# The output projection's products in another order, row sums in small pieces, most output blocks finished on VectorE

## The chip, the core and the metric

The kernel runs on one core of a Trainium2 chip. The core has five engines with a queue of instructions each: TensorE (PE in the profile; its weight loads are PEld), VectorE (DVE), ScalarE (ACT), GpSimd (POOL) and SyncE (SP). DMA transfers are issued from these queues. The metric is the device time of one execution in microseconds; the time before is the median of three runs.

## The reference, cut to what matters

One encoder layer over 1024 new frames of one stream (the prompt tokens) and 16 next frames of 8 running streams (the sample), in float32, model width 2048, eight stick-breaking heads and eight retention heads of 128.

```python
h = rms_norm(x, norm_pre)
q_sb, k_sb, v_sb, gate_sb, q_r, k_r, v_r, gate_r = project(h, w_in, pos)   # 2048 x 8192; rotary on q_r, k_r
o_sb = stick_breaking(q_sb, k_sb, v_sb)            # causal, prompt in blocks of 128, sample over a cache of 1024
o_r, state = retention(q_r, k_r, v_r, state)       # chunks of 64, per-head decay
y = concat(head_rms_norm(o_sb) * g_sb * silu(gate_sb), head_rms_norm(o_r) * g_r * silu(gate_r))
out = einsum('bte,ed->btd', y, w_out)              # 2048 x 2048, the output projection
x = x + rms_norm(out, norm_post)
return x, new keys and values, new states          # for prompt and sample
```

## The kernel before, in words

**Precision.** TensorE multiplies in a reduced float32. Every operand is therefore split: ACT copies it to the reduced type (`hi`, for weights `wh`, L139), DVE subtracts that from the original (`lo`, `wl`, L140), and a product is three matmuls, hi by wh, hi by wl and lo by wh.

**Stages.** The prompt has eight tiles of 128 tokens. Tiles 0–3 and the sample's tile form group 0, tiles 4–7 group 1. For each group the input projections run head by head (L314, L373, L401), in a written order of steps such as ("rk", 6), the retention keys of head 6. Attention and retention of a head are jobs: generators that are advanced by `tick`, one tick for each few matmuls, so that their instructions are mixed into the stream of projections. The number that a job yields is the count of ticks to its next piece. A job `column_sums` prepares sums of output weights in DRAM (`s_t`), a job `row_sums` sums of token operands. `place` keeps an instruction behind the product last issued, in the order that the scheduler then writes; an instruction without it stands where the scheduler puts it. Weights come on SP's queue into four buffers (`wr`), four splits ahead of use at most. Row sums, operand loads, input rows and accumulating outputs go on POOL's queue.

**Output projection.** It is done with seven products in place of eight for a 2 x 2 arrangement of blocks (tokens 0–3 and 4–7 by two columns blocks of 512), with sums of weights and of tokens. A unit is one such arrangement: `half` says which four heads of both branches are summed over, `u` which two column blocks; there are four units. Their seven products are named by digits: "1" uses operand a11 (tokens 0–3, stick-breaking heads), "2" a12 (tokens 0–3, retention heads), "4" a22 (tokens 4–7, retention heads), and "6", "5", "7" and "3" use sums S2, S1, s3 and s4 of such operands. One product is a step: 4 weight blocks by 4 token tiles by 3 matmuls, 48 matmuls of 128 x 512, in four PSUM banks. In all 28 steps (L1285), of which steps 0 and 1 follow the last input projections directly.

Between steps `fill` loads the next operand into a free slot by a 1 MB transfer, and two steps or more later, by the table `due`, `cut` splits it (L1261 on ACT, L1262 on DVE). When a tile of a step is complete, `give` adds its bank to the output blocks (`outs[t][c]`, tile t, column c, 128 x 512): copies on ACT, additions on DVE (L1384, and L1382 where the sign is turned). After its last product, a block is squared on ACT and multiplied by the gain on DVE (L1388). When the sum of squares of a tile is known, `scale` finishes the block: either on DVE (L1398), which multiplies by the scale and adds the input rows `xr` and sends the block by SP, or, where `added` says so, on ACT, with a transfer that adds onto rows which `give_x` has copied to the output before. `finish_first` does this for tokens 0–3; for tokens 4–7 it is done tile by tile as `mixed_last` interleaves the last unit's "7" and "4". `finish_sample` does the sample's rows (L1454): it loads a raw row block `rawc`, waits for its next turn and finishes it. The names `mh`, `ml`, `s3h`, `a22l` and so on in the trace are the hi and lo of operand slots.

The functions that the change touches, and what calls them:

## Time and profile before

| | |
|---|---|
| Time, median of 3 runs | 2340.72 us (2336.19 to 2345.64) |
| Profiled execution, its own time | 2345.99 us |
| Span of its trace | 2344.3 us |
| TensorE busy | 2276.5 us, 97% |
| DVE, ACT, POOL busy | 1410.7, 918.9 and 561.8 us |
| Transfers | 477.25 MB, mean 204 GB/s |

The span runs from the first to the last instruction of the profiled execution. A line such as `PE a L1285 <- DVE wl L140: 6.4, 4, 4.4` says that matmuls of line 1285 into `a` waited 6.4 us in all, 4 times, at most 4.4 us, for line 140 on DVE. In a timeline, each row has its start, its duration, engine, line and operation, output and inputs, and in brackets how long the engine had stood before and what released it. For DMA the last number is the microseconds from issue to landing.

### The profile page before, as it was taken

What the parts mean: (1) busy time and instruction counts of PE and PEld (TensorE: products, weight loads), DVE (VectorE), ACT (ScalarE), POOL (GpSimd) and SP (SyncE); (2) the same over time, 40 slices, a digit from 0 to 9 for tenths busy, and PEclk for the clock granted to TensorE, in tenths of its full rate; (3) what the DMA queues carried; (4) which work ended last, traced back from release to release, by engine and by line L of the source; (5) the groups of instructions that cost most, each with busy time, mean ns of one, the idle gap of its engine ahead of it and who ended that gap; (6) DMA issues with size and microseconds to landing.
All of it is one profiled execution on the core that took longest, in us unless ns stands there. A gap on an engine that the chain in (4) does not pass through costs nothing.

```text
span 2344.3 us, 38591 instructions
## 1 busy us (share of the span) xinstructions
PE 2276.5 (97%) x13920; PEld 2016.2 (86%) x13920; DVE 1410.7 (60%) x2763; ACT 918.9 (39%) x1899; POOL 561.8 (24%) x819
## 2 busy tenths in 40 slices
PE   7999999999999999999999999999998999999994
PEld 7999999999999999998888888888887787888873
DVE  8246564556555563556667766676665556745666
ACT  6323332333333242334443444444443443544333
POOL 2123241414223241313221321122022212100011
PEclk9999999999999999999999999999999999999997
DMA  7659786877869787798968888787769757685576
GB/s 250 158 142 229 167 184 170 189 194 175 203 149 203 173 190 183 175 222 222 219 190 230 243 238 252 232 255 225 230 190 255 195 146 206 237 242 200 170 234 178
DMA packets 702000, 477.25 MB, mean 204 GB/s; under 512 B 234960, under 2 KB 633552, under 8 KB 697200
## 3 DMA queue, kind: packets, MB, share of 16 engines
q1 hardware_dynamic: 623776, 317.32, 52.0%
q0 software_dynamic: 41968, 133.87, 21.7%
q10 hardware_dynamic: 36064, 23.60, 3.4%
q8 instruction: 109, 1.79, 0.3%
q14 instruction: 83, 0.68, 0.1%
HBM read 372.94 MB, written 117.44 MB: 209 GB/s over the span
## 4 chain that ended last, share of the span: by engine, by line
PE 82%; DMA 6%; issue 5%; DVE 4%; ACT 1%; POOL 1%; SPq 0%; DVEq 0%; POOLq 0%; ACTq 0%
PE acc L314 48%; PE accn L373 11%; PE a L1285 7%; PE accx L401 4%; PE pa L711 2%; PE z L678 2%; PE sao L1209 1%; PE pd L847 1%; PE zc L782 1%; DMA ml<-s_y 1%; DMA s_s<-s_S 1%; PE rs L869 1%; DMA be<-s_bd 1%; DMA s_S<-s_S 1%; PE pS L902 1%
## 5 line engine op out<-in xcount | busy, mean ns | idle before, releaser
L314 PE MATMUL acc<-mh,wh 128*128 128x256 f32 (+2 forms) x2304 | 662.1, 340 | 2.8 <-DVE rv L1162 1.8
L314 PE MATMUL acc<-ml,wh 128*128 128x256 f32 (+2 forms) x2304 | 662.8, 340 | 0.8 <-DVE p0u L152 0.8
L314 PE MATMUL acc<-mh,wl 128*128 128x256 f32 (+2 forms) x2304 | 663.5, 340 | 0.0
L140 DVE TENSOR_TENSOR wl<-wr,wh 128x512 fp32r<-128x512 f32 x432 | 296.3, 689 | 427.7 <-ACT wh L139 419.8
L139 ACT ACTIVATE wh<-wr 128x512 fp32r<-128x512 f32 x432 | 272.2, 632 | 588.1 <-PE acc L314 342.9
L314 PEld LDWEIGHTS acc<-mh,wh 128*128 128x128 f32 x2304 | 422.5, 188 | 39.5 <-issue 6.6
L314 PEld LDWEIGHTS acc<-mh,wl 128*128 128x128 f32 x2304 | 422.2, 189 | 36.7 <-issue 8.2
L314 PEld LDWEIGHTS acc<-ml,wh 128*128 128x128 f32 x2304 | 422.2, 188 | 35.9 <-issue 6.6
L763 POOL DMA_DIRECT2D kc<-cache_sb_k x256 | 167.1, 658 | 282.8 <-DVE kcT L794 130.2
L373 PE MATMUL accn<-whn,mh 128*128 128x256 f32 x768 | 223.9, 292 | 0.0
L373 PE MATMUL accn<-wln,mh 128*128 128x256 f32 x768 | 217.1, 283 | 0.0
L373 PE MATMUL accn<-whn,ml 128*128 128x256 f32 x768 | 217.0, 283 | 0.0
L373 PEld LDWEIGHTS accn<-whn,mh 128*128 128x128 f32 x768 | 146.7, 191 | 9.8 <-issue 7.9
L373 PEld LDWEIGHTS accn<-wln,mh 128*128 128x128 f32 x768 | 146.7, 191 | 0.3
L373 PEld LDWEIGHTS accn<-whn,ml 128*128 128x128 f32 x768 | 146.5, 191 | 0.0
L615 DVE TENSOR_TENSOR_SCAN kp<-kp 128x640 f32<-128x640 f32 (+6 forms) x72 | 108.4, 1505 | 37.0 <-POOL kp L604 34.4
L1285 PE MATMUL a<-wh,mh 128*128 128x512 f32 x320 | 124.7, 390 | 2.4 <-DVE o L1384 2.4
L1285 PE MATMUL a<-wl,mh 128*128 128x512 f32 x320 | 125.1, 391 | 1.7 <-DVE wl L140 1.7
L1285 PE MATMUL a<-wh,ml 128*128 128x512 f32 x320 | 125.1, 391 | 0.0
L587 DVE STREAM_TRANSPOSE kp<-be 128x640 f32<-128x640 f32 (+6 forms) x72 | 95.4, 1325 | 8.0 <-DMA be<-s_bd 6.0
L140 DVE TENSOR_TENSOR wln<-wrn,whn 128x512 fp32r<-128x512 f32 x80 | 54.9, 689 | 68.1 <-ACT whn L139 65.2
L139 ACT ACTIVATE whn<-wrn 128x512 fp32r<-128x512 f32 x80 | 50.6, 632 | 115.3 <-PE acc L314 59.2
(268 smaller groups left out, 3588.5 us busy)
## 6 DMA issues: line engine op xcount, KB each, us to landing
wr<-w_in SPq DMA_DIRECT2D x384, 256.0 KB, 4.6
vc<-cache_sb_v SPq DMA_DIRECT2D x64, 512.0 KB, 7.3
wr<-w_out SPq DMA_DIRECT2D x112, 256.0 KB, 4.0
wrn<-w_in SPq DMA_DIRECT2D x80, 256.0 KB, 3.8
kc<-cache_sb_k SPq DMA_DIRECT2D x256, 64.0 KB, 4.3
kc<-cache_sb_k POOLq DMA_DIRECT2D x256, 64.0 KB, 4.6
tr<-w_out SPq DMA_DIRECT2D x32, 512.0 KB, 6.5
s_t<-ts POOLq DMA_DIRECT2D x16, 1024.0 KB, 6.4
```

The lines of the kernel that those rows point to most:

```text
L139: nc.scalar.activation(hi, src, AF.Copy)
L140: nc.vector.tensor_tensor(lo, src, hi.bitcast(F32), ALU.subtract)
L314: last = nc.tensor.matmul(a[:, :m], lhs[:, j, :], rhs[w][:, j, o : o + m], start=(w == 0 and j == 0 and n == 0), stop=(w == KT // WQ - 1 a ...
L373: product[0] = nc.tensor.matmul(a, lhs[q][:, jj, ts], rhs[:, j, :], start=(w == 0 and j == 0 and n == 0 and t % 2 == 0), stop=(w == KT // ...
L401: product[0] = nc.tensor.matmul(banks[t], lhs[q][:, j, ts], rhs, start=(k == 0 and n == 0), stop=(k == KT - 1 and n == 2))
L587: place(nc.vector.transpose(dst.rearrange("p (k b j) -> p k j b", j=4, b=32), raw))
L615: nc.vector.tensor_tensor_scan(rev, rev, rev, 1.0, ALU.mult, ALU.bypass)
L678: mm = nc.tensor.matmul(z[:, :c], q2[a][:, i * P : (i + 1) * P], k2[b][:, :c], start=(m == 0), stop=(m == 2))
L711: nc.tensor.matmul(po[:, :P], at[:, j, :], rest["vn"][:, j, :], start=(j == 0), stop=(j == t))
L763: (nc.gpsimd if i < 2 else nc.sync).dma_start(kc[32 * i : 32 * i + 32, :].rearrange("p (k d) -> p k d", d=32), cache_k[0, 2 * c + j, s * 5 ...
L782: mm = nc.tensor.matmul(z[r, :], qp[:, j, r], ready[2 * j + c // 2][:, c % 2, :], start=(j == 0), stop=(j == 1),)
L1285: product[0] = nc.tensor.matmul(bank, a[:, k, ts], b, start=(name in "125" and k == 0 and n == 0), stop=(k == H // 2 - 1 and n == 2), skip ...
```

## The change

The order of the 28 steps is one list now. The units' products were "1625734", "1265734", "1265734", "1265374", unit after unit. Now the third unit stops after "12653", the fourth does "16532", and then come the third's "7" and "4" and the fourth's "7" and "4", so that the last four steps concern tokens 4–7 alone. The third unit's "7" and "4" start in a bank of their own, for which its "6" is given to three output blocks.

`s_t` is laid out so that one weight block is contiguous (rows of 2 KB one behind the other). `row_sums` goes head by head in pieces of 256 KB, waits for each head to be ended, and starts at head 4's keys in place of head 6's retention keys, 36 ticks between pieces, and for heads 4–7 12 ticks. `cut` is placed. Operand cuts come three steps after the fill. The sample's rows are finished during the second and third units, one turn longer after their load. `added` holds for the first column of tokens 0–3 only (4 blocks, 12 before), the other 28 blocks are finished on DVE; those of tokens 0–3 leave by POOL's queue, those of tokens 4–7 by SP's. The input rows for them come in pieces of 256 KB, five ticks apart.

```diff
 D_CS = 14
+D_RS = (36, 12)
...
-    s_t = [scr.tile([P, H, 4, 512], F32, name=f"s_t{u}") for u in range(2)]
+    s_t = [scr.tile([H, 4, P, 512], F32, name=f"s_t{u}") for u in range(2)]
...
-    UNITS = tuple(zip((0, 0, 1, 1), (0, 1, 0, 1), ("1625734", "1265734", "1265734", "1265374")))
+    STEPS = [(0, s) for s in "1625734"] + [(1, s) for s in "1265734"] + [(2, s) for s in "12653"]
+    STEPS += [(3, s) for s in "16532"] + [(2, s) for s in "74"] + [(3, s) for s in "74"]
...
-            last_load[0] = nc.sync.dma_start(wr, s_t[u][:, k, "5674".index(name), :])
+            last_load[0] = nc.sync.dma_start(wr, s_t[u][k, "5674".index(name)])
...
+            def ended(self):
+                return all("end" in x and x["end"].done for x in (self.rest, self.ret))
...
-                    place(nc.gpsimd.dma_start(s_t[u][:, k], t))
+                    place(nc.gpsimd.dma_start(s_t[u][k].rearrange("f p e -> p f e"), t))
...
-        def row_sums(q):
-            hs, hr = (slice(d * H + q * H // 2, d * H + (q + 1) * H // 2) for d in range(2))
+        def row_sums(q, wait):
+            heads = range(q * H // 2, (q + 1) * H // 2)
             for name, first, more in (
-                ("S2", s_sum["S1"][:, hs, :], s_y[0][:, hs, :NB_TOK]),
-                ("s3", s_y[0][:, hs, :NB_TOK], s_y[1][:, hs, :]),
-                ("s4", s_sum["S2"][:, hs, :], s_y[0][:, hr, :NB_TOK]),
+                ("S2", lambda h: s_sum["S1"][:, h, :], lambda h: s_y[0][:, h, :NB_TOK]),
+                ("s3", lambda h: s_y[0][:, h, :NB_TOK], lambda h: s_y[1][:, h, :]),
+                ("s4", lambda h: s_sum["S2"][:, h, :], lambda h: s_y[0][:, H + h, :NB_TOK]),
             ):
-                place(nc.gpsimd.dma_start(s_sum[name][:, hs, :], first))
-                yield D_TI[1]
-                place(nc.gpsimd.dma_start(s_sum[name][:, hs, :], more, accum_op=ALU.add))
-                yield D_TI[1]
+                for act, src in ((nc.gpsimd.dma_start, first), (add_rows, more)):
+                    for h in heads:
+                        while not ready[h]():
+                            yield 3
+                        place(act(s_sum[name][:, h, :], src(h)))
+                        yield wait
+                made.add((name, q))
+
+        made = set()
+        ready = {}
+
+        def add_rows(dst, src):
+            return nc.gpsimd.dma_start(dst, src, accum_op=ALU.add)
...
                 hi, lo = (x[:, j : j + 2, :NB_TOK] for x in mix[name])
-                nc.scalar.activation(hi, lo.bitcast(F32), AF.Copy)
-                nc.vector.tensor_tensor(lo, lo.bitcast(F32), hi.bitcast(F32), ALU.subtract)
+                place(nc.scalar.activation(hi, lo.bitcast(F32), AF.Copy))
+                place(nc.vector.tensor_tensor(lo, lo.bitcast(F32), hi.bitcast(F32), ALU.subtract))
...
-                if (gi, step, h) == (1, "rk", 6):
-                    run["rows"] = Job(row_sums(0), 2)
+                if (gi, step, h) == (1, "k", 4):
+                    run["rows"] = Job(row_sums(0, D_RS[0]), 2)
...
-            end = n == (2 if t >= 4 and c % 2 == 0 else 4)
+            end = n == (4 if t < 4 else {0: 3, 1: 5, 2: 2, 3: 4}[c])
...
-                nc.vector.scalar_tensor_tensor(o, o, rs, xrs[t, c // 2][:, c % 2 * 512 : (c % 2 + 1) * 512], ALU.mult, ALU.add)
-                nc.sync.dma_start(y_rows(t)[:, cs], o)
+                nc.vector.scalar_tensor_tensor(o, o, rs, xrs[t, c], ALU.mult, ALU.add)
+                (nc.gpsimd if t < 4 else nc.sync).dma_start(y_rows(t)[:, cs], o)
...
-            return c < 2 and t < 6
+            return t < 4 and c == 0
+
+        wanted = [(t, c) for t in range(PT) for c in range(4) if not added(t, c)]
+
+        def load_x(q):
+            for x in "hl":
+                xr = mp.tile([P, 5, 512], F32, name="xr", tag=f"m{x}{q}")
+                for j in range(5):
+                    if wanted:
+                        t, c = wanted.pop(0)
+                        place(nc.gpsimd.dma_start(xr[:, j], x_rows(t)[:, c * 512 : (c + 1) * 512]))
+                        xrs[t, c] = xr[:, j]
+                        yield 5
...
-            for t in range(6):
-                xs_given[t] = nc.scalar.dma_start(y_rows(t)[:, :1024], x_rows(t)[:, :1024])
+            for t in range(4):
+                xs_given[t] = nc.scalar.dma_start(y_rows(t)[:, :512], x_rows(t)[:, :512])
...
                 place(nc.gpsimd.dma_start(xr, xs_flat[:, cs]))
                 yield
+                yield
                 nc.vector.tensor_tensor(raw, raw, gpost[:, cs], ALU.mult)
...
+        banks = {(0, "1"): chain}
+        for step, (n, name) in enumerate(STEPS):
+            half, u = divmod(n, 2)
+            x1, x2 = 2 * u, 2 * u + 1
+            if (n, name) == (0, "2"):
+                job = Job(row_sums(1, D_RS[1]), 96)
+            if (n, name) == (2, "1"):
                 drain(job)
-            if n == 2:
                 given_x = Job(give_x(), 2)
-            pools = (accp, accq) if n % 2 == 0 else (accq, accp)
-            banks = {}
-            for name in names:
-                if step > 1:
-                    banks[name] = (
-                        four(pools[name in "25"]) if name in "125" else banks["1" if name in "674" else "5"]
-                    )
+            if n in (1, 2) and step < 20:
+                next(sample, None)
+            for combo in due.pop(step, ()):
+                cut(combo)
+            if step < 2:
+                continue
+            apart = n == 2 and name in "74"
+            if name in "125" or (apart and name == "7"):
+                pool = accq if name in "257" or n == 1 and name == "1" else accp
+                if n == 1 and name in "25":
+                    pool = accp
+                banks[n, name] = four(pool)
+            bank = banks[n, {"6": "1", "3": "5"}.get(name, name) if name not in "74" else "7" if n == 2 else "1"]
+            to = {"1": [(0, x1)], "2": [(0, x1)], "6": [(0, x2)], "3": [(0, x2)], "7": [(4, x2)], "5": [(4, x2)], "4": [(4, x1)]}
+            to = to[name]
+            if n == 2 and name == "6":
+                to = [(0, x2), (4, x2), (4, x1)]
+            fresh = name in "125" or apart and name == "7"
...
-                if name == "2":
-                    fill("s4", mix["a12"], half, nc.gpsimd)
-                    due.setdefault(step + 3, []).append("s4")
-                elif name == "3" and not final:
-                    fill("a12", mix["s4"], half if u == 0 else 1, nc.gpsimd)
-                    due.setdefault(step + 2, []).append("a12")
-                elif (half, u) == (0, 1):
-                    fill(used, mix[used], 1, nc.gpsimd)
-                    due.setdefault(step + 2, []).append(used)
...
+                    u_ = last_scale(t, c)
+                    for cc in (2, 0, 3, 1):
+                        scale(t, cc, u_)
+
+            if (n, name) == (3, "7"):
+                rest[0] = rest_of()
+                mixed_last("74", banks[3, "1"], last_done)
+                break
+            mixed_product(name, bank, done, fresh=fresh)
+            used = USES[name]
+            later = None
+            if name == "2" and n < 3:
+                later = "s4", mix["a12"], half
+            elif name == "3" and n < 2:
+                later = "a12", mix["s4"], u
+            elif n == 1:
+                later = used, mix[used], 1
+            elif (n, name) == (3, "6"):
+                later = "a12", mix["S2"], 1
+            if later:
+                fill(*later, nc.gpsimd)
+                due.setdefault(step + 3, []).append(later[0])
+            if (n, name) in ((3, "1"), (3, "5"), (3, "3")):
+                Job(load_x({"1": 0, "5": 3, "3": 2}[name]), 2)
+            if (n, name) == (3, "2"):
+                drain(given_x)
+                firsts = Job(finish_first(), 2)
```

What the change moves, at three places.

First, ACT's queue between the last projections and the first output product. `wh` are weight splits, `rg` and `ro` the last head's retention, L1261 (L1275 after the change) is the cut of a11. Before:

```order
L139 ACTIVATE wh<-wr 128x512 [waits DMAHW3_49,PE_49,Activation_49]
L1261 ACTIVATE mh_21434<-ml_21435 128x2x512 [waits DMAHW6_49]
L1261 ACTIVATE mh_21434<-ml_21435 128x2x512
L139 ACTIVATE wh_21555<-wr_21549 128x512 [waits DMAHW4_49,PE_49,Activation_49]
L631 ACTIVATE sq,ssq_21315<-so 128x128 [waits DVE_49,Activation_49]
L139 ACTIVATE wh_21603<-wr_21598 128x512 [waits DMAHW5_49,PE_49,Activation_49]
L417 ACTIVATE rg<-acc_21286 128x512 [waits DMASW3_49,DMASW2_49,PE_49]
L895 ACTIVATE ro<-pa 128x128 [waits DMASW6_49,DMAHW7_49,DVE_49,PE_49]
```

After:

```order
L140 ACTIVATE wh<-wr 128x512 [waits DMAHW3_49,PE_49,Activation_49]
L140 ACTIVATE wh_21573<-wr_21567 128x512 [waits DMAHW4_49,PE_49,Activation_49]
L632 ACTIVATE sq,ssq_21333<-so 128x128 [waits DVE_49,Activation_49]
L140 ACTIVATE wh_21621<-wr_21616 128x512 [waits DMAHW5_49,PE_49,Activation_49]
L418 ACTIVATE rg<-acc_21304 128x512 [waits DMASW5_49,DMASW4_49,PE_49]
L896 ACTIVATE ro<-pa 128x128 [waits DMASW0_49,DMAHW7_49,DVE_49,PE_49]
L632 ACTIVATE sq,ssq_21328<-ro 128x128 [waits DVE_49]
L140 ACTIVATE wh_21653<-wr_21648 128x512 [waits DMAHW2_49,PE_49]
L1275 ACTIVATE mh_21452<-ml_21453 128x2x512 [waits DMAHW6_49]
L1275 ACTIVATE mh_21452<-ml_21453 128x2x512
```

The cut has moved behind two more weight splits, `rg` and a copy of `ro`.

Second, POOL's queue around the sums of heads 0–3 during head 6. L1246 and L1248 are the row sums (128x2048 and 128x4x512 are 1 MB), the rest is attention. Before:

```order
L1246 DMA s_S_109<-s_S_108 128x2048 [waits DMASW7_49]
L574 DMA s_be_6_19666<-be 128x28x32 [waits DMASW0_49,DVE_49]
L581 DMA be<-s_be_5_19534 128x6x128 [waits DMASW2_49]
L604 AFFINE_SELECT kp<-kp 128x128 [waits DVE_49,Activation_49]
L604 AFFINE_SELECT be<-be 128x128 [waits DMASW3_49,Activation_49]
L1248 DMA s_S_109<-s_y_104 128x4x512 [waits DMASW7_49]
L581 DMA be<-s_be_6_19666 128x7x128 [waits DMASW0_49]
L574 DMA s_rk_6_19813<-rk 128x16x32 [waits DMASW4_49,DVE_49]
L1246 DMA s_s_110<-s_y_104 128x4x512 [waits DMASW5_49]
L1248 DMA s_s_110<-s_y_105 128x2048 [waits DMASW6_49,DMASW5_49]
```

After, where L1254 and L1262 are the row sums (128x512 is 256 KB):

```order
L1254 DMA s_s_111<-s_S_109 128x512
L575 DMA s_be_6_19682<-be 128x28x32 [waits DMASW0_49,DVE_49]
L582 DMA be<-s_be_5_19550 128x6x128 [waits DMASW2_49,DMASW1_49]
L1254 DMA s_s_111<-s_S_109 128x512
L604 AFFINE_SELECT kp<-kp 128x128 [waits DVE_49,Activation_49]
L604 AFFINE_SELECT be<-be 128x128 [waits DMASW3_49,Activation_49]
L582 DMA be<-s_be_6_19682 128x7x128 [waits DMASW0_49]
L1254 DMA s_s_111<-s_S_109 128x512 [waits DMASW4_49]
L575 DMA s_rk_6_19830<-rk 128x16x32 [waits DMASW5_49,DVE_49]
L1254 DMA s_s_111<-s_S_109 128x512 [waits DMASW6_49]
L1262 DMA s_s_111<-s_y_104 128x512 [waits DMASW7_49]
```

Of the 24 pieces for heads 0–3 only the last eight start here; the 16 others stand further ahead on POOL's queue.

Third, DVE's queue in the third unit's "7" and "4", the 25th and 26th step. L1413 are scales, L1397 gives, L1403 gains, L141 weight splits. After:

```order
L1413 SCALAR_TENSOR_TENSOR o_2_21856<-o_2_21856,outr,xr 128x512 [waits DMASW5_49]
L1413 SCALAR_TENSOR_TENSOR o_3_21864<-o_3_21864,outr,xr 128x512 [waits DMASW6_49]
L1397 SCALAR_TENSOR_TENSOR o_1_21880<-a_23835,o_1_21880 128x512 [waits PE_49]
L1397 SCALAR_TENSOR_TENSOR o_1_21881<-a_23836,o_1_21881 128x512 [waits PE_49]
L1397 SCALAR_TENSOR_TENSOR o_1_21882<-a_23837,o_1_21882 128x512 [waits PE_49]
L1403 TENSOR_TENSOR o_1_21880<-o_1_21880,gpost 128x512 [waits Activation_49]
L1397 SCALAR_TENSOR_TENSOR o_1_21883<-a_23838,o_1_21883 128x512 [waits PE_49]
...
L1413 SCALAR_TENSOR_TENSOR o_2_21857<-o_2_21857,outr,xr 128x512 [waits DMASW0_49]
L1413 SCALAR_TENSOR_TENSOR o_3_21865<-o_3_21865,outr,xr 128x512 [waits DMASW1_49]
L141 TENSOR_TENSOR wl_23984<-wrt,wh_23983 128x512 [waits DMAHW7_49]
```

Before, at the corresponding place between the fourth unit's "5" and "3":

```order
L1384 TENSOR_TENSOR o_3_21849<-a_23773,o_3_21849 128x512 [waits PE_49]
...
L1384 TENSOR_TENSOR o_3_21852<-a_23776,o_3_21852 128x512 [waits PE_49]
L1454 TENSOR_TENSOR rawc<-rawc,gpost 128x512 [waits DMASW2_49,DMASW0_49,DVE_49]
L140 TENSOR_TENSOR wl_23924<-wr_23921,wh_23923 128x512 [waits DMAHW3_49,Activation_49]
L1455 SCALAR_TENSOR_TENSOR rawc<-rawc,smpr,xrc 128x512 [waits DMASW1_49,DVE_49]
L140 TENSOR_TENSOR wl_23963<-wrt,wh_23962 128x512 [waits DMAHW4_49,Activation_49]
L140 TENSOR_TENSOR wl_23969<-wrt,wh_23968 128x512 [waits DMAHW5_49,Activation_49]
L1454 TENSOR_TENSOR rawc<-rawc,gpost 128x512 [waits DMASW7_49,DMASW5_49,DVE_49]
L1384 TENSOR_TENSOR o_3_21845<-a_23773,o_3_21845 128x512 [waits PE_49]
```

The sample's two raw row blocks that stood ahead of weight splits and gives are gone from the end; four gives, four gains and three scales stand ahead of one weight split instead.

More of the change, by code (lines that the diff above doesn't have):

```diff
@@ L1253, in fill @@
             mix[name] = pair
+            assert name not in ("S2", "s3", "s4") or (name, q) in made
             src = {"a11": s_y[0][:, h0], "a12": s_y[0][:, h1], "a22": s_y[1][:, h1]}
@@ L1286, in mixed_step @@
                     bank, a[:, k, ts], b,
-                    start=(name in "125" and k == 0 and n == 0), stop=(k == H // 2 - 1 and n == 2),
+                    start=(fresh and k == 0 and n == 0), stop=(k == H // 2 - 1 and n == 2),
                     skip_group_check=True,
@@ L1299, in mixed_last @@
         def mixed_last(two, banks, done):
-            kept = [mp.tile([P, 4, 512], F32R, name=f"w{x}", tag=f"m{x}2") for x in "hl"]
+            kept = [mp.tile([P, 4, 512], F32R, name=f"w{x}", tag=f"m{x}1") for x in "hl"]
             blocks = [list(mixed_blocks()), list(mixed_blocks(keep=kept))]
@@ L1316, in tile_hybrid_step @@
                 heads.append(Head(gi, h, last))
+                ready[h] = heads[-1].ended
                 last = heads[-1]
@@ L1459, in tile_hybrid_step @@
         due = {2: ["S1"], 4: ["s3"], 5: ["a22"]}
-        step = 0
         sample = finish_sample()
-        for n, (half, u, names) in enumerate(UNITS):
-            final = n == 3
-            if n == 0:
-                job = Job(row_sums(1), 100)
-            if n == 1:
+        banks = {(0, "1"): chain}
[5 more added lines that the diff above has]
+            if (n, name) == (2, "1"):
@@ new lines, in tile_hybrid_step, with done @@
+            bank = banks[n, {"6": "1", "3": "5"}.get(name, name) if name not in "74" else "7" if n == 2 else "1"]
[4 more added lines that the diff above has]
+            fresh = name in "125" or apart and name == "7"
+            def done(p):
+                for base, c in to:
+                    give(base + p, c, bank[p])
@@ new lines, in last_done @@
+            def last_done(name, p):
+                t = 4 + p
+                c = {"7": x2, "4": x1}[name]
+                give(t, c, banks[3, "1"][p])
+                if name == "7":
+                    more_of(t, c)
+                else:
+                    u_ = last_scale(t, c)
[5 more added lines that the diff above has]
+                break
```

56 lines of the change are left out of this document (7 added, 49 removed).

## The prediction

> **What bounds the kernel now.** I read the engine sums first, then what TensorE waits for over the whole execution, then single stretches around those waits, then the end.
>
> ```profile
> span 2344.3 us, 38591 instructions
> PE 2276.5 (97%) x13920; PEld 2016.2 (86%) x13920; DVE 1410.7 (60%) x2763; ACT 918.9 (39%) x1899; POOL 561.8 (24%) x819
> ...
> PE a L1285 <- DVE wl L140: 6.4, 4, 4.4
> PE pa L711 <- DVE kp L587: 6.0, 2, 5.2
> PE pa L887 <- DVE sc L871: 5.7, 1, 5.7
> PE a L1285 <- DVE o L1384: 2.4, 1, 2.4
> PE a L1285 <- DVE o L1382: 2.3, 1, 2.3
> ```
>
> TensorE is busy 2276.5 of 2344.3 us, so it is the bound, and since the change keeps all 28 steps of 48 output matmuls it can only win from the other 67.8 us. The waits (engine, line, waited for: us in total, times, longest) are few and long. One follows the start, which is not touched; the five shown are all in the stretch that the change rewrites. The second part of the 67.8 us is the end:
>
> ```profile
> 2321.19 0.40 PE L1285 MATMUL a<-wh,a22l 128*128 128x512 f32 x1
> ...
> 2322.00:2344.30 22.30, 0.00 (x0) 0.00 (x0) 8.55 (x19) 1.62 (x6) 1.73 (x2) 0.56 0.98 258
> ```
>
> The last matmul ends at 2321.59 (2321.19 + 0.40), so 22.7 us pass without TensorE. In that window (span, then busy us of PE, weight load, DVE, ACT, POOL, then granted clock, DMA share, GB/s) DVE works 8.55 us but the DMA engines are 98% busy: the end waits for transfers. That leaves 45.1 us of gaps.
>
> A long gap costs more than itself. Around the wait on `sc`:
>
> ```profile
> 1984.76 0.80 PE L887 MATMUL pa<-rv,sc 128*128 128x128 f32 x2 [5.67 <-DVE sc L871]
> ...
> 1987.06 0.63 PE L314 MATMUL acc<-mh,wl 128*128 128x512 f32 x1
> 1987.49 0.63 PE L314 MATMUL acc<-mh,wh 128*128 128x512 f32 x1
> ...
> 1990.35 0.40 PE L314 MATMUL acc<-mh,wh 128*128 128x512 f32 x1
> 1990.58 0.39 PE L314 MATMUL acc<-ml,wh 128*128 128x512 f32 x1
> ```
>
> After 5.67 us idle, matmuls start 0.43 us apart (1987.06 to 1987.49), and 0.23 apart from 1990.35 on. About 13 of them (5.6 us at 0.43) lose 0.2 each: some 2.6 us more. The Trainium skill ("TensorE: Matmul & The Clock Gate", Part 1) has the clock halve after an idle window of about 3.4 us; the trace agrees, since after the wait of 2.38 us quoted below nothing slows.
>
> **The change part by part.**
>
> *1. The first cut no longer blocks* (cuts are placed behind work already issued).
>
> ```profile
> 1979.33 2.00 ACT L1261 ACTIVATE mh<-ml 128x1024 fp32r<-128x1024 f32 x2 [8.16 <-DMA ml<-s_y]
> 1980.42 2.36 DVE L1262 TENSOR_TENSOR ml<-ml,mh 128x1024 fp32r<-128x1024 f32 x2 [8.40 <-ACT mh L1261]
> 1984.44 0.27 DVE L871 TENSOR_TENSOR sc<-rs,dT 128x128 f32<-128x128 f32 x1
> ```
>
> ACT stood 8.16 us at the head of its queue for the operand's transfer, with the last retention copies and splits behind it; DVE stood behind ACT, `sc` behind DVE, TensorE behind `sc`. In the changed order the cut stands behind `rg`, `ro` and two weight splits on ACT and behind `sc` on DVE, so the transfer has time to land while TensorE goes on projecting. The wait goes with its slow stretch: −5.67 − 2.6 = **−8.3**. The cut itself then becomes due at product "1", some 24 matmuls later (24 × 0.23 = 5.5 us against 2.0 us of ACT); if it is late by the rest I lose up to 4, so −8.3 to −4.
>
> *2. Row sums in 256 KB pieces, from head 4 on instead of head 6.*
>
> ```profile
> 1764.00:1842.00 78.00, 70.75 (x326) 57.79 (x325) 40.15 (x63) 26.90 (x52) 18.65 (x21) 0.96 0.87 225
> ...
> wr<-w_in SPq DMA_DIRECT2D x8, 256.0 KB, 10.0
> s_s<-s_y POOLq DMA_DIRECT2D x3, 1024.0 KB, 9.1
> ...
> wr<-w_in SPq DMA_DIRECT2D x384, 256.0 KB, 4.6
> ...
> 1809.14 0.63 ACT L139 ACTIVATE wh<-wr 128x512 fp32r<-128x512 f32 x1 [9.56 <-DMA wr<-w_in]
> ```
>
> While five 1 MB sums go out, weights land 10.0 us after issue instead of the usual 4.6, ACT's split waits 9.56 us for one, and TensorE idles 7.25 of 78 us; with the longest gap (5.2, on `kp`) a slow stretch as above, 2.5: 9.8 us at stake. Afterwards this stretch holds four copies and one sum of 256 KB, a quarter of the bytes. But attention's own transfers stay, and `kp` waits for those: I take −6, between 0 and −9.8.
>
> The pieces go instead between 1588, where head 4's keys are projected, and 1764:
>
> ```profile
> 1600.00:1700.00 100.00, 97.67 (x466) 81.43 (x465) 67.19 (x120) 42.38 (x88) 19.62 (x23) 0.98 0.78 231
> ```
>
> There TensorE idles 2.33 in 100 us with the DMA share at 0.78. Some 4 MB over 176 us add about 23 GB/s to 231: no burst, but POOL queues and weights stand closer. I charge **+2**, from 0 to one burst of 9.8.
>
> *3. Input rows for the end: 28 loads of 256 KB, five ticks apart, for 10 of 512 KB in pairs.*
>
> ```profile
> 2276.28 0.63 ACT L139 ACTIVATE wh<-wr 128x512 fp32r<-128x512 f32 x1 [5.05 <-DMA wr<-w_out]
> 2277.80 1.06 POOL L1524 DMA_DIRECT2D xr<-x_prompt  x2
> 2278.38 0.47 PE L1285 MATMUL a<-wh,mh 128*128 128x512 f32 x1 [2.38 <-DVE o L1384]
> ```
>
> Here a weight came 5.05 us late, splits and gives behind it, and TensorE lost 2.38. Spread loads leave the weight its share: **−1.5** (0 to −2.4).
>
> *4. The sample's rows are finished in the second and third units.*
>
> ```profile
> 2291.87 0.69 DVE L1454 TENSOR_TENSOR rawc<-rawc,gpost 128x512 f32<-128x512 f32 x1 [6.38 <-DMA rawc<-s_raw]
> 2298.84 0.80 PE L1285 MATMUL a<-wl,s3h 128*128 128x512 f32 x1 [4.40 <-DVE wl L140]
> ```
>
> DVE stood 6.38 us for one raw row; four gives, their gains and the weight splits queued behind it, and TensorE waited 4.40 plus about 2.2 slow. The loads now go out two steps (2 × 11 us) ahead of their use, past no full queue, against 4 to 6 us of landing: **−6.6**. If one is late in the earlier units it costs that much again there, in place of here.
>
> *5. The wait before the last tile's "4"* (2.28, next row) came from DVE, in arrears with the scales of tokens 0–3 (second row) when it owed the give. Those scales end a step and a half earlier now: **−2.0**, 0 at worst.
>
> ```profile
> 2318.52 0.50 PE L1285 MATMUL a<-wh,a22h 128*128 128x512 f32 x1 [2.28 <-DVE o L1382]
> ...
> L1398 DVE SCALAR_TENSOR_TENSOR o<-o,lastu,xr 128x512 f32<-128x512 f32 x12 | 8.3, 745 | 0.1
> L1388 DVE TENSOR_TENSOR o<-o,gpost 128x512 f32<-128x512 f32 x12 | 8.1, 681 | 0.2
> L1382 DVE SCALAR_TENSOR_TENSOR o<-a,o 128x512 f32<-128x512 f32 x8 | 5.5, 687 | 2.7 <-PE a L1285 2.7
> ```
>
> *6. The end.*
>
> ```profile
> DMA packets 4609, 8.40 MB, mean 245 GB/s; under 512 B 512, under 2 KB 512, under 8 KB 4608
> ...
> out<-o SPq DMA_DIRECT2D x20, 256.0 KB, 11.0
> out<-o POOLq DMA_DIRECT2D x12, 256.0 KB, 13.8
> ...
> DMA to landing us min/median/max: 2.5/11.0/13.2
> ...
> wr<-w_out SPq DMA_DIRECT2D x112, 256.0 KB, 4.0
> ...
> 2327.95 2.74 DVE L1398 SCALAR_TENSOR_TENSOR o<-o,lastu,xr 128x512 f32<-128x512 f32 x4
> ```
>
> All 32 output blocks leave after 2310, 8.4 MB at 245 GB/s, and land 11.0 to 13.8 us after issue (SP's between 2.5 and 13.2). DVE is through at 2330.7 (2327.95 + 2.74), 9.1 after the last matmul, so 13.6 of the 22.7 us is transfer. Tokens 0–3 now leave some 17 us earlier, while "7" and "4" of the last unit run, and only 16 blocks remain. DVE then sets the end: 9.1 as now, plus up to four scales of tokens 4 and 5 that ACT did before, of which about 2 us are not yet done at the last matmul: 11.2. A 256 KB transfer among spread ones lands in 4.0, and issue and closing take about 0.7 (13.6 less the longest landing of 13.2, and a little for the issue). Sum 15.9: **−6.8**. Bounds: 9.1 and the shortest landing, 2.5, with 0.4 behind it give −10.7; as transfer-bound as now gives 0.
>
> *7. A new wait.* In "4" of the third unit DVE gets four gives (0.69), four gains (0.68) and three scales (0.745) ahead of the second weight split, some 7.5 us at the pitch of such rows, begun when the first tile of "7" is complete, so 5.9 us run on after "7" ends; in the changed order TensorE has 20 matmuls before it needs that split, 20 × 0.23 = 4.6. **+1.3**, too short for a slow stretch; 0 to 5 if the scales' x rows are late.
>
> *8. Pinned cuts.* The five later cuts (about 4.2 us of ACT, 4.9 of DVE each) now stand at a place in the order:
>
> ```profile
> L1261 ACT ACTIVATE mh<-ml x28: 1040/1051/1074, 1979.3 to 2261.6; 128x1024 fp32r<-128x1024 f32 x28
> L1262 DVE TENSOR_TENSOR ml<-ml,mh x28: 1212/1218/1227, 1980.4 to 2262.9; 128x1024 fp32r<-128x1024 f32 x28
> ```
>
> They come a step later than before (due +3), covered by the 11 us of the step ahead. Where weight splits queue behind them, each may cost 0 to 1.5: **+2** of 0 to 5.
>
> The weight sums in contiguous rows cost nothing that I can find: their writes spread to 512 rows of 2 KB on the same queue, off TensorE's path, and the reads (256 KB either way) land ahead of use. The eight extra gives (8 × 0.69 = 5.5 us of DVE) are spread over the third unit's 55 us ahead of its "7".
>
> Sum: −8.3 −6 +2 −1.5 −6.6 −2.0 −6.8 +1.3 +2 = **−25.9**. The profiled execution took 2345.99 (span 2344.3 and 1.7 around it), so 2320.1 by its terms. It lies 5.3 above the median of 2340.72; part of its waits will be smaller in a usual run, so I take −23.5 from the median: **2317**.
>
> **The rivals.**
>
> *A. Congestion only moves.* Nothing is gained at the old burst and one stall of 9.8 appears at 1588–1764 where I charged 2. For it: DMA share 0.78 there, 0.87 now. Against: sums are a quarter as big and paced. −25.9 + 6 + 7.8 = −12.1: 2328.6 from the median.
>
> *B. The end stays transfer-bound* because tokens 0–3 go through POOL's queue and run into tokens 4–7's blocks: 22.7 again. For it: share 0.98 now. Against: half of the bytes leave a step earlier. −19.1: 2321.6.
>
> *C. Small transfers are dear.* By the rows, 48 pieces at 4.6 (a 256 KB weight) take 221 us of landing on POOL's queue against 12 × 9.1 = 109. If that makes the operands late at the five later cuts, 2 us each: 2325. The Trainium skill ("DMA: Bandwidth & Descriptors", Bandwidth) advises transfers of 1 MiB or more, and its fit (Anatomy of one DMA) of 2.0 us plus bytes at 436 GB/s makes an estimate of 125 us for the pieces against 53. It speaks against this part of the change; no run so far shows which holds.
>
> *D. Slower: weights starve for heads 4 to 7.* The sums of heads 4–7, the column sums and attention's transfers meet between 1588 and 1764, and four projections wait a weight as at 1809: 4 × 9.8 = 39 over the −21.9 that the sum has without part 2 and its charge: 2358. It decides from four such stalls on; three leave it within the noise. Against: the share of 0.78 leaves room, and weights are loaded four ahead.
>
> **How the numbers follow.** Forecast .64, A .15, B .12, C .05, D .04. This kernel's runs tell about 0.5% (11.7 us) from no change: faster is under 2329.0, slower over 2352.4. The forecast, B and C are faster but for .05 of their spread, A is half and half, D is slower: faster .84, same .12, slower .04. The low end adds the far bounds of parts 2, 3, 6, 7 and 8 (−3.8, −0.9, −3.9, −1.3, −2) and half of the charge in 2: 2304; the high end takes in A: 2333.
>
> **What would show it.** The wait of `pa` on `sc` is gone (1). The stretch before the last head's retention idles under 3 us and 1600–1764 no more than now (2). No DVE wait on `rawc` reaches TensorE (4). A wait on `wl` of 1 to 2 us appears in "4" of the third unit (7). From the last matmul to the end pass about 16 us, DVE busy for 11 of them, blocks on SP's queue landing in about 4 (6). It is wrong if the x rows or POOL's queue hold up the scales, so that DVE reaches the final gives late, or if heads 4–7 show ACT waiting for `wr` by 9 us.

## The result, and the profile after

The changed kernel takes 2329.01 us (median of six runs, 2322.92 to 2333.13) against 2344.57 for the kernel before: a ratio of 0.9938, interval 0.9920 to 0.9955. That is 0.6% faster, inside the stated range, but 14 to 16 us won where 23.5 were forecast.

The profiled execution, its sums and the longest of TensorE's waits, without the one at the start that the change does not touch (engine, line waited for: us in total, times, longest):

```profile
span 2327.8 us, 38668 instructions
PE 2273.1 (98%) x13920; PEld 2013.1 (86%) x13920; DVE 1420.7 (61%) x2777; ACT 912.9 (39%) x1889; POOL 596.2 (26%) x876
```

```profile
PE acc L315 <- DVE rv L1166: 4.9, 1, 4.9
PE a L1299 <- ACT mh L1275: 4.4, 4, 1.6
PE pd L834 <- DVE kp L588: 4.3, 4, 2.8
PE a L1299 <- DVE ml L1276: 3.3, 5, 1.6
PE a L1299 <- ACT wh L140: 2.9, 2, 2.4
PE pa L712 <- DVE kp L588: 1.5, 2, 1.3
PE a L1299 <- DVE wl L141: 1.4, 2, 1.0
```

The waits on `sc`, on the gives and the 4.4 on `wl` are gone, and the wait of `pa` on `kp` has fallen from 6.0 to 1.5. In their place stand 4.9 on `rv` (1.8 before), and 7.7 (4.4 + 3.3) on `mh` and `ml`, the cuts. Two windows beside those of before (columns as there), the stretch of the old burst and the end:

```profile
1764.00:1842.00 78.00, 76.70 (x367) 64.14 (x366) 49.51 (x76) 34.50 (x68) 23.09 (x29) 1.00 0.80 210
2313.50:2327.80 14.30, 0.04 (x1) 0.00 (x0) 9.70 (x22) 1.13 (x4) 0.00 (x0) 0.59 0.61 206
```

TensorE idles 1.3 us there, 7.25 before. At the end DVE works 9.7 of 14.3 us and the DMA share is 0.61, where it was 0.98: the end is DVE's now. The groups of output transfers in the last 65 us say the same, with the last number the median landing:

```profile
out<-o POOLq DMA_DIRECT2D x16, 256.0 KB, 7.1
out<-o SPq DMA_DIRECT2D x16, 256.0 KB, 2.7
```

Added up from the gaps of over 0.3 us in both traces, the 16.5 us between the two spans come from these places:

| Place | idle before | idle after | change |
|---|---|---|---|
| start and attention, to 1640 | 17.7 | 20.3 | +2.6 |
| wait on `rv` near 1650, and what follows | 2.3 | 4.9 | +2.6 |
| heads 6 and 7, 1764 to 1975 | 7.9 | 1.3 | −6.6 |
| `sc` near 1980 | 5.7 | 0 | −5.7 |
| output steps with their cuts, 1980 to 2260 | 2.0 | 8.7 | +6.7 |
| last steps | 9.1 | 4.3 | −4.8 |
| last matmul to the end | 22.7 | 14.2 | −8.5 |
| TensorE busy (slow clock) | 2276.5 | 2273.1 | −3.4 |

What is missing to 16.5 lies in shorter gaps. The first row concerns work that the change does not touch; its longest waits (2.8 us here, near 232) differ from one trace below to the next. The 8.7 of the cuts are the 7.7 on `mh` and `ml` and 1.0 at the cut of `s3`, which the profile puts down to issue, that is, to nothing that it shows.

### The profile page after: what moved, and what is told of

It reads as the page before. It is cut to its first block, busy times and chain, and to the rows that moved or that the text cites. A ratio compares the mean times of both kernels' runs of the same rounds, so it can differ in the third digit from the quotient of the medians.

```text
span 2327.8 us, 38668 instructions
## 1 busy us (share of the span) xinstructions
PE 2273.1 (98%) x13920; PEld 2013.1 (86%) x13920; DVE 1420.7 (61%) x2777; ACT 912.9 (39%) x1889; POOL 596.2 (26%) x876
## 4 chain that ended last, share of the span: by engine, by line
PE 86%; DVE 5%; DMA 4%; issue 1%; ACT 1%; SPq 1%; POOL 0%; DVEq 0%; ACTq 0%; POOLq 0%
PE acc L315 47%; PE a L1299 11%; PE accn L374 11%; PE accx L402 4%; PE pa L712 3%; PE z L679 2%; PE sao L1213 2%; PE pd L848 1%; DMA be<-s_bd 1%; PE zc L783 1%; DMA wr<-w_in 1%; DVE kp L588 1%; DVE o L1413 1%; PE rs L870 1%; PE pa L888 1%
## 5 line engine op out<-in xcount | busy, mean ns | idle before, releaser
L141 DVE TENSOR_TENSOR wl<-wr,wh 128x512 fp32r<-128x512 f32 x432 | 296.9, 689 | 432.9 <-ACT wh L140 421.9
L141 DVE TENSOR_TENSOR wln<-wrn,whn 128x512 fp32r<-128x512 f32 x80 | 54.9, 688 | 68.1 <-ACT whn L140 65.6
```

The lines of the kernel that those rows point to most:

```text
L141: nc.vector.tensor_tensor(lo, src, hi.bitcast(F32), ALU.subtract)
```

## The experiments

Times are medians in us; each group of experiments was timed beside fresh runs of the kernel before (2345 to 2347), and ratios are to those. Line numbers are each kernel's own.

### The cuts: not placed, and placed half a step ahead

```diff
-                place(nc.scalar.activation(hi, lo.bitcast(F32), AF.Copy))
-                place(nc.vector.tensor_tensor(lo, lo.bitcast(F32), hi.bitcast(F32), ALU.subtract))
+                nc.scalar.activation(hi, lo.bitcast(F32), AF.Copy)
+                nc.vector.tensor_tensor(lo, lo.bitcast(F32), hi.bitcast(F32), ALU.subtract)
```

> The changed kernel with its cuts no longer placed. My theory: placing the cuts removed the 8.16 us stand of ScalarE at the first cut and the 5.67 us wait on sc with its slow stretch (8.3 together), but the pinned later cuts cost 7.7 us of TensorE waits on mh and ml. So without placing, the wait on sc comes back (5 to 6 us, and 2 to 2.6 of slow clock), the waits on mh and ml from 2045 on (5.5 us) vanish, and the time is 1 to 5 us above the changed kernel (2329): 2330 to 2334. Rival: the waits on mh and ml are work that is late for another reason (the operand's transfer, a backlog of VectorE); then they stay, and the time is 8 us up: 2337.

Measured: 2325.26, ratio 0.9912 (0.9885 to 0.9939). Waits of TensorE:

```profile
PE acc L315 <- DVE rv L1166: 5.2, 1, 5.2
PE a L1299 <- DVE o L1399: 3.8, 1, 3.8
PE pa L888 <- DVE sc L872: 3.7, 1, 3.7
```

As expected `sc` comes back, with 3.7 instead of 5.7, and all waits on `mh` and `ml` disappear. A new one of 3.8 appears at a later loose cut, where ACT stood 6.48 us for an operand's transfer. Even so this kernel is 4 us below the changed one, not above it. Their intervals overlap, so I claim only that placing the cuts brought nothing by itself.

The other edit keeps `place`, but gives the cuts of the next step to a job inside the step before:

```diff
+            if step + 1 in due:
+                cutting = Job(cuts_of(due.pop(step + 1)), 14)   # one 128x1024 piece every 8 matmuls
```

> The changed kernel with its cuts still placed, but the later ones issued piece by piece as a job in the middle of the step before (from 14 matmuls on, 8 matmuls apart) instead of at the step's boundary. My theory: the waits on mh and ml from 2045 on (5.5 us) are only the place of the cut; they vanish, and so 4 to 6 us are won: 2323 to 2325. Rival: the operand's transfer has not landed half a step earlier, so the cuts then hold up the weight splits behind them, the same microseconds appear as waits on wh or wl, and the time is 2328 to 2332.

Measured: 2319.99, ratio 0.9888 (0.9861 to 0.9915), below the changed kernel's interval and 3 us below what I expected. First the changed kernel's timeline at the cut of two operands ahead of the sixth step, then the waits that are left with cuts ahead:

```profile
2047.26 1.99 ACT L1275 ACTIVATE mh<-ml 128x1024 fp32r<-128x1024 f32 x2
2048.35 0.50 PE L1299 MATMUL a<-wh,mh 128*128 128x512 f32 x1 [0.76 <-ACT mh L1275]
2050.76 2.35 DVE L1276 TENSOR_TENSOR ml<-ml,mh 128x1024 fp32r<-128x1024 f32 x2
2052.04 1.21 PE L1299 MATMUL a<-wh,ml 128*128 128x512 f32 x4 [1.58 <-DVE ml L1276]
```

```profile
PE a L1308 <- ACT mh L1275: 1.7, 1, 1.7
...
PE a L1308 <- DVE ml L1276: 0.5, 1, 0.5
```

ACT did not stand for a transfer at 2047: the operand was there, the instruction's place was late. Nine us are won. The waits of the later cuts, 6.5 us in the changed kernel, are gone; the rest is not traced to one place. The rival, that loads were not there half a step earlier, falls.

Of the cuts only the first (1.7 and 0.5) still waits, and not for its load. The edit moves the cuts in `due` alone, and the first, of a11, is not among them. In the changed kernel, where it stands at the same place:

```profile
ml<-s_y SPq DMA_DIRECT2D x1, 1024.0 KB, 8.1
...
1981.70 0.63 ACT L140 ACTIVATE wh<-wr 128x512 fp32r<-128x512 f32 x1 [3.78 <-PE acc L315]
1982.23 1.99 ACT L1275 ACTIVATE mh<-ml 128x1024 fp32r<-128x1024 f32 x2
1983.33 0.50 PE L1299 MATMUL a<-wh,mh 128*128 128x512 f32 x1 [1.63 <-ACT mh L1275]
```

The load was issued at 1965.0 and landed 8.1 us later, at 1973.1, nine us ahead of the cut. What stood before the cut in ACT's queue was a weight split that waited 3.78 us for the last projection's products. Issuing this cut earlier too was not tried.

The kernel before with `place` at its cuts alone, the first diff of this section the other way round:

> The kernel before with its cuts placed, nothing else changed. My theory: the wait on sc goes (5.67 and 2.6 of slow clock), the first cut costs 2 us where it now stands, later cuts cost about 5 at the boundaries of steps, where due times come only two steps after the fill. So the gain is 0 to 4: 2341 to 2345 beside 2344.6. Rival: placing costs nothing and wins the whole 8.3: 2336.

Measured: 2343.10, ratio 0.9987 (0.9972 to 1.0002), no difference. Its waits:

```profile
PE a L1285 <- DVE ml L1262: 8.0, 3, 5.9
...
PE pa L887 <- DVE sc L871: 0.4, 1, 0.4
```

`sc` falls from 5.7 to 0.4, and 8.0 comes on `ml`, with 2.7 on `mh`. The longest, 5.9, is a cut held in DVE's queue behind a raw row of the sample that had not landed. Such a row already cost 4.4 in the kernel before, through `wl`, a wait that is gone here; so I read most of the 5.9 as that wait in another place, not as a price of placing. The other 4.8 are the first cut (1.9 and 0.5) and the later ones, and they take back most of what `sc` gives.

### The row sums as before

`row_sums` of the kernel before, in the changed one:

```diff
-                if (gi, step, h) == (1, "k", 4):
-                    run["rows"] = Job(row_sums(0, D_RS[0]), 2)
+                if (gi, step, h) == (1, "rk", 6):
+                    run["rows"] = Job(row_sums(0), 2)      # the old function, 1 MB a transfer
...
-                job = Job(row_sums(1, D_RS[1]), 96)
+                job = Job(row_sums(1), 100)
```

> The changed kernel with the row sums as before: 1 MB transfers from head 6's retention keys on. My theory: the early small sums won the congestion of heads 6 and 7 (9 us of waits and slow clock before, 1.3 after) and gave 3 to 5 us back at the sample's wait on rv (1.82 before, 4.91 after). So with the old sums the wait on kp near 1800 comes back with 5 us or more, the one on rv near 1650 falls under 2.5, and the time is 3 to 7 us above the changed kernel: 2332 to 2336. Rival one: the rv wait has nothing to do with the sums and varies from execution to execution; then it stays near 5 and the time is 7 to 10 up. Rival two: the congestion near 1800 is attention's own traffic; then kp's wait stays near 1.3 and the time stays within 2 us of 2329.

Measured: 2337.15, ratio 0.9963 (0.9947 to 0.9978), 6 to 8 us above the changed kernel; the two intervals just touch.

```profile
PE pa L712 <- DVE kp L588: 5.7, 2, 5.2
...
PE acc L315 <- DVE rv L1166: 0.2, 1, 0.2
```

By the medians, the sums' part of the change is worth 6 to 8 us net. The trace of this kernel does not add up to that. It is of the fastest of ten executions (2331.55), only 2.0 us longer than the changed kernel's; among the differences are 3.9 more at `kp`, 2.0 more at `sc` and 4.7 less at `rv`. What fills the other executions is not traced. That the burst comes back is clear, in the stretch of the two windows above:

```profile
1764.00:1842.00 78.00, 72.03 (x332) 59.57 (x330) 40.02 (x63) 28.61 (x55) 17.74 (x20) 0.96 0.91 235
```

TensorE idles 6.0 us there, 1.3 in the changed kernel, and weights issued from 1790 to 1812 land in 12.9 us in place of 7.9. The edit undoes size, start and spacing of the sums together, so it does not show which of them counts. All traces agree on `kp`: with 1 MB sums the longest wait of `pa` on it is 5.1 to 5.4 in four kernels, with small ones 0.9 to 1.5 in nine and none of note in the tenth. How `rv` gets late in the changed kernel is seen in one window and one row of its timeline:

```profile
1640.00:1660.00 20.00, 15.09 (x63) 12.55 (x62) 7.79 (x16) 4.64 (x11) 4.54 (x5) 0.85 0.99 266
```

```profile
1653.29 0.63 ACT L140 ACTIVATE wh<-wr 128x512 fp32r<-128x512 f32 x1 [6.35 <-DMA wr<-w_in]
```

The DMA share is 0.99 (0.80 before in the same window), a weight split waits 6.35 us for its load, and `rv` stands behind it on DVE.

### The sample's rows late, and early in the kernel before

In the changed kernel the sample is finished in the last unit again, one turn after each load:

```diff
-            if n in (1, 2) and step < 20:
-                next(sample, None)
+            if n == 3:                 # after the step's product, and one yield in finish_sample
+                next(sample, None)
```

> The changed kernel with the sample's rows finished as before: in the last unit's steps, used one turn after their load. My theory: the wait of VectorE on rawc blocked gives and weight splits there and cost TensorE 4.40 and 2.2 of slow clock before; it comes back, 3 to 7 us: 2332 to 2336. Rival: in the new order these rows come a step and a half earlier beside the input rows, and the loads land in time: 2327 to 2331.

Measured: 2329.14, ratio 0.9932 (0.9910 to 0.9953): nothing. DVE stands 4.08 and 2.46 us for two of the raw rows, but none of these waits reaches TensorE.

In the kernel before, the sample in the third unit instead of the fourth:

```diff
-                if final:
+                if n == 2:
                     next(sample, None)
```

> The kernel before with the sample's rows finished in the third unit instead of the fourth. My theory: the wait of 4.40 with its slow stretch in the last unit goes, with a small return in the third (VectorE waits for a raw row there without a queue of gives): 3 to 6 us won: 2339 to 2342 beside 2345. Rival: the wait only moves to the third unit with the row: 2344 to 2346.

Measured: 2336.93, ratio 0.9969 (0.9953 to 0.9986), 7 to 9 us faster, more than the 3 to 6 expected. The longest wait on `wl` falls from 4.4 to 1.6:

```profile
PE a L1285 <- DVE wl L140: 3.0, 4, 1.6
...
PE a L1285 <- DVE o L1382: 1.3, 1, 1.3
```

The two runs go together: the sample's rows did cost the kernel before what I said, but putting them back into the last unit of the changed kernel costs nothing. So something else in the change removes that wait as well, and undoing one of two sufficient causes shows nothing. What the other is was not tried; I take it to be the order, by which the steps of the fourth unit come earlier, or the spread loads of input rows. It is not that the rows land in time: in the kernel before with early rows DVE stands 4.5, 3.8 and 4.3 us for them. What differs is what stands behind them in DVE's queue.

### The end: the old order, the adding transfers, and both

Old order of the last steps, rest as changed:

```diff
-    STEPS += [(3, s) for s in "16532"] + [(2, s) for s in "74"] + [(3, s) for s in "74"]
+    STEPS += [(2, s) for s in "74"] + [(3, s) for s in "1653274"]
```

> The changed kernel with the third unit's 7 and 4 directly after its 3, that is unit after unit as before (the last unit is 1653274). My theory: the end's gain came from tokens 0-3 leaving two steps earlier: then 8.4 MB leave in the last 35 us again, the last matmul to the end takes 18 to 21 us in place of 14.2, and VectorE is in arrears at the last gives by 2 us: 2334 to 2338. Rival: the gain at the end came from fewer transfers that add in memory (4 for 12), not from the order: the end stays at 14 to 15.5 and the time at 2328 to 2331.

Twelve blocks finished on ACT and added in memory, rest as changed (`give_x` copies the rows for them again):

```diff
-            return t < 4 and c == 0
+            return c < 2 and t < 6
```

> The changed kernel with 12 blocks again finished on ScalarE and added in memory (columns 0 and 1 of tiles 0 to 5; 20 blocks on VectorE). My theory: with tokens 0-3 out of the way, the end depends on VectorE's work behind the last matmul (11 us), which gets shorter by up to two scales of tile 4 and 5 that lie before it, while an adding transfer lands in 4 to 7 in place of 2.7: end 13 to 16, time 2327 to 2332, no change. Rival: the adding transfers were what made the end transfer-bound: end 18 to 21, time 2333 to 2337.

Both edits together:

> The changed kernel with both the old order of the last units (the third unit's 7 and 4 directly after its 3) and 12 blocks added in memory. Each alone left the end short (13.6 and 12.6 us after the last matmul, against 22.7 in the kernel before). Theory now: the end was transfer-bound only while both held, the adding transfers spreading over the time in which all 32 blocks leave; with both back the end takes 18 to 22 us and the blocks land in 7 us or more on SP's queue: 2333 to 2340. Rival: what shortened the end is that tokens 0-3 leave on another queue (POOL's) than tokens 4-7; that is kept here, and the end stays at 13 to 15: 2328 to 2333.

Measured: old order 2329.84, ratio 0.9937 (0.9917 to 0.9956); twelve added 2332.90, 0.9946 (0.9931 to 0.9961); both 2334.71, 0.9962 (0.9950 to 0.9974). The windows from the last matmul to the end, of these three kernels in turn:

```profile
2314.70:2328.30 13.60, 0.00 (x0) 0.00 (x0) 9.03 (x20) 1.13 (x4) 0.00 (x0) 0.63 0.72 265
```

```profile
2322.40:2335.00 12.60, 0.03 (x1) 0.00 (x0) 8.47 (x19) 1.13 (x4) 0.00 (x0) 0.63 0.73 222
```

```profile
2311.60:2336.10 24.50, 0.01 (x1) 0.00 (x0) 10.00 (x23) 2.97 (x8) 5.09 (x7) 0.60 0.96 247
```

And the group of SP's output transfers of the last:

```profile
out<-o SPq DMA_DIRECT2D x12, 256.0 KB, 11.2
```

Each edit alone leaves the end at 13.6 and 12.6 us, as short as the 14.2 of the changed kernel; both together make it 24.5, with a DMA share of 0.96 and blocks landing in 11.2 us. My theory, that the order shortens the end, falls in the form in which I stated it, and so does its rival, that only the number of adding transfers does: one of the two edits suffices. The queue of tokens 0–3 is POOL's in all three, so it does not shorten the end by itself. In the median both edits together cost some 6 us, less than the 10 at the end: the last matmul ends 2 us earlier there, and the profiled execution is 3 us longer than the median.

The order does something else. With the old order alone TensorE waits once more before the last tile's "4":

```profile
2309.20 0.80 PE L1299 MATMUL a<-wh,a22h 128*128 128x512 f32 x1 [3.97 <-DVE o L1397]
```

DVE is in arrears with the scales of tokens 0–3, 12 of 16 its own now (with both edits, where ACT has twelve blocks again, this wait is not there). The new order moves that work away from the end. Against this it has waits of 0.5, 1.0 and 2.4 in the third unit's "4" and ahead of the last "7", which the old order does not have. The two orders come to the same time when few blocks are added in memory.

### The weight sums' layout

```diff
-    s_t = [scr.tile([H, 4, P, 512], F32, name=f"s_t{u}") for u in range(2)]
+    s_t = [scr.tile([P, H, 4, 512], F32, name=f"s_t{u}") for u in range(2)]   # and its write and read to match
```

> The changed kernel with the weight sums laid out as before (written with rows of 8 KB per partition, read with rows of 2 KB 64 KB apart). Theory: writing lands 0.5 us earlier (6.5 for 7.0) and reading lands as now, both ahead of use, so nothing moves: 2326 to 2332. Rival: contiguous blocks make the weights' loads land earlier in the busy last steps, and without them waits on wh and wl grow by 3 us or more: 2332 to 2336.

Measured: 2330.38, ratio 0.9939 (0.9920 to 0.9959): no difference. Reads land in 3.4 us, in the changed kernel in 3.5; writes in 6.9 and 7.0, so the 0.5 us that I expected there did not come.

### Versions with the cuts ahead

Cuts ahead, and the row sums begun later and closer together:

```diff
-D_RS = (36, 12)
+D_RS = (26, 12)
...
-                if (gi, step, h) == (1, "k", 4):
+                if (gi, step, h) == (1, "sg", 4):
```

> The changed kernel with the cuts issued in the step before (which took 9 us off it) and the row sums begun one step later (after the projection of values of heads 4 and 5, 26 ticks apart in place of 36). Theory: the wait on rv near 1650, 3.5 to 6.3 us in six executions with early sums and 0 to 3.4 in four with late ones, comes from row and weight sums that meet the weights' loads between 1636 and 1647; without sums there it falls to 0 to 2.5, and the sums still end before head 7, so kp's wait near 1800 stays under 1.5: 2315 to 2318. Rival: the denser sums bring the wait on kp back with 3 to 5 us: 2319 to 2323.

Measured: 2321.94, ratio 0.9910 (0.9891 to 0.9928). The time is the rival's, but not by its mechanism: `kp` does not come back, and the wait on `rv` falls to 2.7, near what I expected. Cuts ahead, the weight sums' old layout as above, and the blocks of tokens 0–3 further apart:

```diff
                     scale(t, c, rs[:, t : t + 1])
-                    yield 5
+                    yield 6
```

> The changed kernel with the cuts issued in the step before, the weight sums laid out as before, and the blocks of tokens 0-3 sent every 6 matmuls in place of 5. Theory: the wait on rv needs both the early sums and the new layout's writes (3.5 to 6.3 with both in seven executions, under 0.4 with either of the two undone in one execution each), so it is under 2 here; the wait before the last 7 (1.8 to 2.4) falls under 1.5 with the blocks spread; 3 to 5 us under the version with cuts ahead alone (2320): 2315 to 2318. Rival: the rv wait varies by itself and comes back with 3 us or more, and the whole stays at 2319 to 2322.

Measured: 2322.92, ratio 0.9906 (0.9890 to 0.9922), 4 us and more above what I expected. The wait before the last "7" is 1.6, not under 1.5. The waits of both versions on `rv`, in this order:

```profile
PE acc L315 <- DVE rv L1166: 2.7, 1, 2.7
```

```profile
PE acc L315 <- DVE rv L1166: 6.1, 1, 6.1
```

The second disproves the part that I had given the layout. Over all traces, early sums have 3.5 to 6.3 in eight kernels and 0.4 in one (the old layout alone), a later start 2.7, the old sums 0.2 to 3.4 in four. Early sums make this wait longer as a rule; what decides in a single execution stays open. Neither version is better than cuts ahead alone (2319.99), which beats the kernel before by 1.1% and the changed one by 0.5%.

## Why the prediction was right and wrong

**The whole.** Faster was right, and the time lies in the range, 12 us above the forecast. Some 4 of the 12 come from the starting point: further runs put the kernel before at 2344.57, not at the 2340.72 that I subtracted from. Between the two traces 16.5 us were won of the 25.9 that I added up. It is close to the 2328.6 of rival A, but not for A's reason: the gain at the old burst was there in full.

**Part 1 and part 8, the cuts,** are the step that failed. I booked −8.3 for `sc` and +2 for the later cuts, "covered by the 11 us of the step ahead". The `sc` wait did go, but a placed cut stands behind the *last* product issued, and the step ahead is then almost over: nothing covers it. For the first cut I counted 24 matmuls of cover; it started at 1982.23, after TensorE had run dry at 1981.70, because one of the weight splits that I had put ahead of it had to wait for the products themselves. The first cut cost 2.2, with 3.4 us of slow clock behind it, and the later ones 6.5, against 0 (at worst 4) and 2 in the prediction. Together the two parts are worth nothing measurable: undone they lose nothing (2325.3), done alone they win nothing (2343.1). The cover that I named is real only where the cut is issued in the middle of the step, which wins 9 us.

**Part 2, the row sums,** was right in kind: −6 and +2 booked. The old burst lost 6.6 us of idling, though eight small pieces and not the five that I counted still fall into it, and by the medians the whole is worth 6 to 8 us net. The charge for the new place was right in size (+2.6 at `rv`), but the clock is slow there for 6.8 us, 3.4 before, and the sign that I named, 1600–1764 idling no more than before, did not come. Rivals A and D, congestion that only moves or starves several heads, did not come: one head paid.

**Part 3, the input rows.** The wait of 2.38 is gone. No run undoes it alone.

**Part 4, the sample,** was right for the kernel before (7 to 9 us alone, 6.6 booked), but is no gain of its own in the changed kernel, where the wait is gone without it. I summed terms that overlap.

**Part 5.** Gone, as booked (−2.0 for 2.3), and by the cause named: with the old order alone it is back with 4.0, since DVE then has more of these scales than in the kernel before.

**Part 6, the end.** Booked 15.9, measured 14.2; DVE is through 10.1 us after the last matmul (2313.54 to 2323.68, the end of its last row below), against 11.2 booked, and the rest is one landing and the close:

```profile
2320.94 2.74 DVE L1413 SCALAR_TENSOR_TENSOR o<-o,lastu,xr 128x512 f32<-128x512 f32 x4
```

The landings of the line that sends the blocks, both queues together:

```profile
DMA to landing us min/median/max: 2.4/2.8/8.4
```

The bound was right. The cause that I named was one of two: tokens 0–3 leaving early suffices, and so do four adding transfers in place of twelve. Rival B, a transfer-bound end, would have come true only without both.

**Part 7.** 1.3 booked, 0.5 and 1.0 measured, at the place named. What I did not see is its sequel 12 us later:

```profile
2291.26 0.63 ACT L140 ACTIVATE wh<-wrt 128x512 fp32r<-128x512 f32 x1 [2.11 <-DMA wrt<-s_t]
2293.07 0.50 PE L1299 MATMUL a<-wh,s3h 128*128 128x512 f32 x1 [2.41 <-ACT wh L140]
```

The weights of the last "7" land late while the blocks of tokens 0–3 leave. It costs 2.4 here, 0.8 to 2.1 in kernels with the same order and the same number of added blocks.

**Rival C and the advice on large transfers.** The sums in 256 KB pieces each land in 3.6 to 11.8 us near 1640 and nobody waits for them. The Trainium skill ("DMA: Bandwidth & Descriptors", Bandwidth) asks for 1 MiB or more per transfer; here the kernel with 1 MB sums is 6 to 8 us slower. Those runs moved and spaced the sums as well, so the size alone is not shown to do it. I take it that what counts here is how long a weight stands behind the sums: in the old burst 12.9 us with the large ones, 7.9 with the small.

## What to carry to other kernels

An instruction pinned behind "the last work issued" at a boundary has no cover: issue it inside the step ahead, where its data have landed and its engine is idle. Before adding up the gains of several edits, ask for each wait which of the edits removes it; where two do, the second may be worth nothing. Bulk transfers that nobody waits for went better in small, spaced pieces here; look for what else is loaded in the places they move to.

## What the runs showed of the hardware

The slow clock needs less idle time than I took. Four windows of the changed kernel, each behind a wait or a pair of waits of TensorE: 4.9 on `rv`; 1.6 and 0.5 at the first cut; 0.5 and 1.0 in the third unit's "4"; 2.4 ahead of the last "7" (granted clock is third from the end):

```profile
1653.80:1660.60 6.80, 5.57 (x19) 5.00 (x20) 3.21 (x9) 2.24 (x8) 0.00 (x0) 0.50 0.91 260
1984.90:1988.30 3.40, 3.33 (x10) 1.92 (x9) 3.40 (x6) 2.63 (x6) 0.00 (x0) 0.50 0.97 343
2280.80:2284.20 3.40, 3.40 (x15) 2.77 (x16) 3.40 (x6) 0.00 (x0) 1.45 (x3) 1.00 1.10 266
2293.00:2297.00 4.00, 3.58 (x14) 2.65 (x15) 4.00 (x9) 2.90 (x9) 0.00 (x0) 1.00 0.18 61
```

After 4.9 us of idling the clock is halved for 6.8 us, and after two waits of only 1.6 and 0.5 for 3.4. After the other two it is full. The kernel with the weight sums' old layout has the same waits of 0.5 and 1.0 in the same "4", 0.6 us earlier, and there it is halved:

```profile
2280.80:2284.20 3.40, 3.40 (x10) 2.66 (x9) 3.15 (x6) 0.00 (x0) 1.75 (x4) 0.50 1.06 299
```

In all traces a slow stretch between the start and the last matmul lasts 3.4 or 6.8 us, once 10.2. The Trainium skill ("TensorE: Matmul & The Clock Gate", Part 1) speaks of one idle window of about 3.4 us, and I had found the trace of before to agree, by its waits of 5.67 and 2.38. That was too quick: in that trace itself the 1.8 us on `rv` were followed by 3.4 us at half clock (0.91 on average from 1640 to 1660). Neither the length of one wait nor the waits added up decide, since the same two had both outcomes; what does is not shown here.
